# Two-layer attention and feed-forward kernel: in the first layer and in the memory heads, each head transposes its own 64 columns instead of two heads sharing one transpose of 128

## The chip, the cores and the metric

The kernel runs on one core of a Trainium2 chip. The metric is the device time of one execution in microseconds (us); less is better. The profile comes from one execution, and its rows name the engines: PE is TensorE (matmuls and transposes), PEld its weight load, DVE is VectorE, ACT is ScalarE, POOL is GpSimd, SP is the engine that issues most DMAs.

## What is computed

Two transformer layers over 1024 positions of width 1024, all in float32. The first layer ("fox") has 12 causal heads of 64 columns with a decay term, the second ("mla") 12 causal heads of 96 columns; each layer has 4 more heads that attend to a memory of 256 rows. Cut to what the change touches:

```python
def fox_mixer(p, b_f, q_gain, k_gain):
    q, k, v, f = jnp.split(p, [MIX_WIDTH, 2 * MIX_WIDTH, 3 * MIX_WIDTH], axis=-1)
    q = rmsnorm(to_heads(q, N_MIX_HEADS), q_gain) * HEAD_DIM ** -0.5
    k = rmsnorm(to_heads(k, N_MIX_HEADS), k_gain)
    log_f = jax.nn.log_sigmoid(f.astype(jnp.float32) + b_f.astype(jnp.float32))
    cum = lax.cumsum(log_f, axis=1).transpose(0, 2, 1)
    return from_heads(causal_block_attention(q, k, to_heads(v, N_MIX_HEADS), cum))

def memory_cross(qm, k_mem, v_mem, q_gain, k_gain):
    q = rmsnorm(qm.reshape(b, s, N_MEM_HEADS, HEAD_DIM), q_gain) * HEAD_DIM ** -0.5
    k = rmsnorm(k_mem, k_gain)
    ...
# per layer: x = x + concat([o_mix, o_mem]) @ w_out; x = x + conv_ffn(rmsnorm(x), ...)
```

## The kernel before

A float32 product is made of float32r pieces: an operand is split into a high part (a cast) and a low part (operand minus high part), and a product takes two or three matmuls. In a layer the order is: projections, attention, output projection, feed-forward part.

After the projections the queries and keys of two neighbouring heads lie side by side in one tile: `q` and `k` are 128 positions by (8 blocks x 128 columns), columns 0 to 63 of a block belonging to the even head and 64 to 127 to the odd one; `mq` is the same for a pair of memory heads. The scores need them transposed, as QA and KA (high part) and QB and KB (low part), 64 rows by 1024 positions. Each head's `prep` does it in two halves of 512 positions:

- An even head (`load_pair`, `odd` = 0) transposes 4 blocks of 128 x 128 into one PSUM tile `psX`; rows 0 to 63 of it are its own, rows 64 to 127 are the next head's. L519 copies rows 64 to 127 to SBUF, back into the tile that was just read (ScalarE in the first layer, VectorE in the second).
- An odd head reads that copy and transposes nothing.
- `split_T` then scales by the gain: L524 (ScalarE) writes the high part, L525 (VectorE, scalar_tensor_tensor) the low part. For an even head both read `psX`, for an odd head the SBUF copy. The copies are recorded at L83 (ScalarE) and L85 (VectorE), the lines of the helper `copy`.

`psX` is a pool of three PSUM banks. The pass that finds each query's largest score (`maxpass`) uses the same three: PE writes a chunk of scores to `psX`, VectorE reduces it (L299, or L304 with the causal mask) into `mA`, PE transposes `mA`, VectorE negates it into `mrow` (L312) and a DMA puts it into QA. A bank is free again only when VectorE has read it. The score and value matmuls use other banks (`psS`, `psO`); GpSimd subtracts `plo` = `pf` - `ph` (L90) for the low part of the probabilities.

`attention` runs head after head; the preparation and max pass of the next heads are woven between the matmuls of the present one, a pair at a time (`TIMES`). At the end of a pair VectorE takes the reciprocal of the row sums (L394, `rec`), DMAs write it to DRAM and read it back on all partitions (`rrow`), and VectorE multiplies the pair's output by it (L93, `oh`). Each engine works its own queue in order. A scheduler places the instructions of the first layer's attention on each queue; in the second layer's attention PE's order is pinned to the program's.

Of the kernel before, what the change touches and what calls it, by code (L numbers as in the profile page):

```python
# [17 lines left out]
P = 128  # L18
# [7 lines left out]
HD = 64  # L26
# [48 lines left out]
def hybrid_kernel(ctx: ExitStack, tc: tile.TileContext, A, out):  # L75
# [5 lines left out]
    def copy(eng, o, i):  # L81
        if eng == "a":
            nc.scalar.copy(o, i)  # L83
        elif eng == "v":
            nc.vector.tensor_copy(o, i)  # L85
        else:
            nc.gpsimd.tensor_copy(o, i)

    def sub(eng, o, a, b):
        (nc.vector if eng == "v" else nc.gpsimd).tensor_tensor(o, a, b, op=OP.subtract)  # L90
# [14 lines left out]
    def transpose(*a, **k):  # L105
        r = nc.tensor.transpose(*a, **k)  # L106
        return late(r) if pin[0] else r
# [17 lines left out]
    def psX():  # L125
        return psum.tile([P, 512], F32, name="psX", tag="X", bufs=3)
# [19 lines left out]
    def late(ins):  # L146
        return tc.keep_in_program_order(ins)
# [5 lines left out]
    ident = const.tile([P, P], F32, name="ident")  # L153
# [52 lines left out]
    def gc(key, n):  # L206
        i = GC[key]
        return g_cols[0:n, i:i + 1]
# [60 lines left out]
    pl = Pools()  # L269
# [215 lines left out]
    class Head:  # L485
        rows_eng = "vv"
        o = {}
# [13 lines left out]
    def load_T(src, Th, Tl, tl0, tl1, gcol, n, half):  # L501

        px = psX()
        for i in range(4):
            transpose(px[:n, i * P:(i + 1) * P], src(half * 4 + i), ident)
        split_T(px[:n, :], Th, Tl, tl0, tl1, gcol, n, half)

    def load_pair(T, odd, Th, Tl, tl0, tl1, gcol, half):

        hs = slice(half * 512, half * 512 + 512)  # L510
        if odd:
            px = T[0:HD, hs]
        else:
            px = psX()
            for i in range(4):
                t = half * 4 + i
                transpose(px[:, i * P:(i + 1) * P], T[:, t * P:(t + 1) * P], ident)
            copy("v" if pl.layer else "a", T[0:HD, hs], px[HD:P, :])
            px = px[0:HD, :]  # L519
        split_T(px, Th, Tl, tl0, tl1, gcol, HD, half)  # L520

    def split_T(px, Th, Tl, tl0, tl1, gcol, n, half):
        hs = slice(half * 512, half * 512 + 512)
        nc.scalar.activation(Th[0:n, hs], px, AF.Identity, scale=gcol)  # L524
        nc.vector.scalar_tensor_tensor(Tl[tl0:tl1, hs], px, gcol, Th[0:n, hs].bitcast(F32),  # L525
                                       op0=OP.mult, op1=OP.subtract)

    def dup(dst, src):
        nc.sync.dma_start(dst.bitcast(F32), src.bitcast(F32))

    class FoxHead(Head):
# [7 lines left out]
        def prep(self):  # L539
            self.qk_tiles()  # L540
            o = (self.row % 2) * HD
            q, k = self.p
            QA, KA, QB, KB = self.QA, self.KA, self.QB, self.KB

            def qt(half):
                load_pair(q, self.row % 2, QA, QB, 0, 64, gc("fox_q", HD), half)
                if half:
                    dup(QB[64:128, :], QA[0:64, :])

            def kt(half):  # L550
                if not half:
                    dup(KA[64:66, :], self.cum[self.row:self.row + 1])
                load_pair(k, self.row % 2, KA, KB, 64, 128, gc("fox_k", HD), half)
                if half:
                    dup(KB[0:64, :], KA[0:64, :])

            def vs():
                self.vh, self.vl = pl.vtile()
                v = self.pv.rearrange("p (t j) -> p t j", t=NT)[:, :, o:o + HD]
                copy("a", self.vh[:, :, 0:64], v)  # L560
                sub("p" if self.row < 2 else "v", self.vl, v, self.vh[:, :, 0:64].bitcast(F32))

            return [lambda: kt(0), lambda: qt(0), lambda: kt(1), lambda: qt(1), vs]
# [14 lines left out]
    class MemHead(Head):  # L578
# [8 lines left out]
        def prep(self):  # L587
            h = self.h
            q = self.mq[h // 2]
            if self.L:  # L590
                T = pl.qk[h // 2]
                self.QA, self.KA, self.QB, self.KB = T[h % 2], mk[0][:, h], T[2 + h % 2], mk[1][:, h]
                if h not in pl.mem_rows:
                    pl.mem_rows.add(h)
                    copy("p", self.QA[64:66, :], ones1[64:66, 0:1].to_broadcast([2, S]))
            else:
                self.qk_tiles()
            QA, KA, QB, KB = self.QA, self.KA, self.QB, self.KB

            def qt(half):  # L600
                load_pair(q.rearrange("p t d -> p (t d)"), h % 2, QA, QB, 0, 64, gc(f"mem_q{self.L}", HD), half)
                if half:
                    dup(QB[64:128, :], QA[0:64, :])

            def kt():
                g = gc(f"mem_k{self.L}", HD)
                px = psX()
                for t in range(2):
                    transpose(px[:64, t * P:(t + 1) * P], kmem[:, t, h * HD:(h + 1) * HD], ident)
                nc.scalar.activation(KA[0:64, :MEM], px[:64, :256], AF.Identity, scale=g)  # L610
                nc.vector.scalar_tensor_tensor(KB[64:128, :MEM], px[:64, :256], g, KA[0:64, :MEM].bitcast(F32),
                                               op0=OP.mult, op1=OP.subtract)
                if self.L:
                    copy("p", KA[64:67, :MEM], ones1[64:67, 0:1].to_broadcast([3, MEM]))
                copy("p", KA[64:66, :MEM], zero1[64:66, 0:1].to_broadcast([2, MEM]))
                dup(KB[0:64, :MEM], KA[0:64, :MEM])

            return [lambda: qt(0), kt, lambda: qt(1)]

        def v(self, kt):  # L620
# [110 lines left out]
    class FFN:  # L731
# [388 lines left out]
        def down(self, s, k, i, finish):  # L1120
# [13 lines left out]
            for u in range(4):  # L1134
# [5 lines left out]
                if i == N - 1 and u % 2:  # L1140
# [13 lines left out]
    Th, Tl = zip(*((hp.tile([P, ND, P], F32R, name=f"hTh{t}"), hp.tile([P, ND, P], F32R, name=f"hTl{t}"))  # L1154
                   for t in range(NT)))
# [264 lines left out]
    Th, Tl, lat, xt = {}, {}, {}, {}  # L1420
# [258 lines left out]
    for g in range(1, 6):  # L1679
        p = groups[g].pieces()  # L1680
# [37 lines left out]
    for j in range(6):  # L1718
        i, x = divmod(t0 + 0.1 + 0.28 * j, 1.0)
# [48 lines left out]
```

## Time and profile before

| | |
|---|---|
| time, median of 3 runs | 2527.79 us (2522.3 to 2529.79) |
| the profiled execution's own time | 2524.59 us |
| its span, first to last instruction | 2522.8 us |
| mean granted TensorE clock, share of full speed | 0.970 |
| attention of the first layer | about 268 to 512 us |
| attention of the second layer | about 1367 to 1765 us |

The profiled execution's time is its span and 1.8 us around it. A change is to be read against the stage where it happens: the two attention stages are about a quarter of the span, and the rest is projections and feed-forward work that the change does not touch.

### The profile page before, as it was taken

The numbers are of one execution on the slowest core, as the hardware profiler recorded it, in microseconds if no ns is written. First come the engines' busy times: TensorE is split into PE (matmuls) and PEld (weight loads), VectorE is DVE, ScalarE is ACT, GpSimd is POOL, SyncE is SP. The second block draws the span as 40 slices with busy tenths as digits, with TensorE's granted clock in tenths as the row PEclk, the third lists the DMA queues.
The fourth block names the chain that finished last, engine by engine and source line by source line (L and its number), as shares of the span: only waits on it lengthen the run. The fifth ranks groups of instructions, "written<-read, shape, count | busy, mean of one in ns | idle before, by whom it ended". The sixth has DMA issues, their size and how long they took to land.

```text
span 2522.8 us, 32481 instructions
## 1 busy us (share of the span) xinstructions
PE 2369.9 (94%) x11609; PEld 1954.7 (77%) x11609; DVE 1892.6 (75%) x3183; ACT 1209.5 (48%) x2341; POOL 985.3 (39%) x640
## 2 busy tenths in 40 slices
PE   7999899998999999989998798889979999998999
PEld 7999666677788888868888576767868888886887
DVE  7432677757778878789997868774488788778997
ACT  5544678723444444434454555555244444443443
POOL 1221467743233233234332566666132333233342
PEclk9999899999999999999999899989989999999999
DMA  4221121253132232451230101010512222226221
GB/s 143 84 51 27 35 61 47 52 177 109 51 92 76 84 92 76 161 190 52 99 134 11 34 23 27 19 38 22 192 56 84 87 81 84 83 85 242 84 101 67
DMA packets 163651, 208.89 MB, mean 83 GB/s; under 512 B 11175, under 2 KB 124682, under 8 KB 163490
## 3 DMA queue, kind: packets, MB, share of 16 engines
q1 hardware_dynamic: 162054, 206.63, 25.9%
q8 instruction: 92, 1.51, 0.2%
q14 instruction: 69, 0.57, 0.1%
q10 hardware_dynamic: 1436, 0.18, 0.0%
HBM read 153.34 MB, written 39.98 MB: 77 GB/s over the span
## 4 chain that ended last, share of the span: by engine, by line
PE 73%; DVE 17%; issue 3%; DMA 3%; POOL 2%; ACT 2%; SPq 0%; DVEq 0%; ACTq 0%; POOLq 0%
PE psX L102 32%; PE psS L102 25%; PE psO L102 14%; DVE f_op L90 2%; PE psX L106 2%; POOL f_op L90 1%; DVE mA L299 1%; DVE psX L304 1%; DVE f_x L1143 1%; DVE KB L525 1%; DVE f_T L90 1%; DMA rrow<-rec 1%; DVE f_d L90 1%; DVE QB L525 1%; DVE f_S L90 1%
## 5 line engine op out<-in xcount | busy, mean ns | idle before, releaser
L90 POOL TENSOR_TENSOR f_op<-f_S,f_op 128x512 fp32r<-128x512 f32 x184 | 272.0, 1479 | 671.0 <-ACT f_op L83 613.7
L102 PE MATMUL psS<-f_T,f_op 128*128 128x512 f32 x1584 | 382.4, 393 | 7.8 <-DVE f_T L90 5.9
L90 POOL TENSOR_TENSOR plo<-pf,ph 128x1024 fp32r<-128x1024 f32 (+2 forms) x160 | 315.1, 1980 | 158.0 <-ACT pf L343 95.7
L102 PEld LDWEIGHTS psS<-f_T,f_op 128*128 128x128 f32 x1584 | 297.0, 189 | 68.9 <-DVE f_T L90 6.5
L102 PE MATMUL psX<-f_B,f_op 128*128 128x512 f32 x1260 | 296.3, 389 | 0.1
L83 ACT CAST f_op<-f_S 128x512 fp32r<-128x512 f32 x248 | 153.6, 621 | 279.0 <-PE psS L102 109.2
L102 PEld LDWEIGHTS psX<-f_B,f_op 128*128 128x128 f32 x1260 | 236.4, 188 | 49.6 <-issue 0.5
L102 PE MATMUL psS<-f_op 128*128 128x512 f32 x960 | 222.4, 390 | 0.4 <-DVE f_op L90 0.4
L102 PEld LDWEIGHTS psS<-f_op 128*128 128x128 f32 x960 | 180.7, 188 | 39.0 <-DVE f_op L90 1.2
L102 PE MATMUL psX<-f_op 128*128 128x512 f32 x666 | 175.3, 403 | 20.8 <-DVE f_op L90 18.1
L102 PE MATMUL psX<-w_w,hTh 128*128 128x384 f32 (+2 forms) x672 | 167.8, 333 | 2.2 <-ACT hTh L83 2.2
L102 PEld LDWEIGHTS psX<-f_op 128*128 128x128 f32 x666 | 127.9, 194 | 54.0 <-DVE f_op L90 24.2
L898 DVE SCALAR_TENSOR_TENSOR f_v<-f_cv,cw,f_v 128x1023 f32<-128x1023 f32 x88 | 150.9, 1715 | 7.6 <-ACT f_v L896 6.2
L342 ACT ACTIVATE ph<-psS 128x1024 fp32r<-128x1024 f32 (+2 forms) x131 | 112.4, 858 | 90.4 <-PE psS L102 83.4
L83 ACT CAST f_op<-f_raw 128x512 fp32r<-128x512 f32 x148 | 91.4, 621 | 132.3 <-PE psS L102 67.1
L102 PE MATMUL psX<-KA,QA 66*128 66x128 f32 (+4 forms) x320 | 111.0, 395 | 24.5 <-DVE mA L299 10.5
L83 ACT CAST f_op<-f_d 128x512 fp32r<-128x512 f32 x144 | 84.3, 619 | 102.0 <-PE psS L102 35.6
L858 DVE TENSOR_TENSOR f_u<-psS,f_p 128x512 f32<-128x512 f32 x44 | 30.4, 691 | 126.7 <-PE psS L102 126.7
L102 PEld LDWEIGHTS psX<-w_w,hTh 128*128 128x128 f32 x672 | 120.8, 190 | 3.2 <-ACT hTh L83 2.8
L898 DVE SCALAR_TENSOR_TENSOR f_v<-f_cg,cw,f_v 128x1023 f32<-128x1023 f32 x88 | 112.6, 1279 | 11.2 <-ACT f_v L896 11.2
L90 POOL TENSOR_TENSOR f_op<-f_d,f_op 128x512 fp32r<-128x512 f32 x52 | 75.3, 1448 | 115.9 <-ACT f_op L83 115.9
L102 PE MATMUL psS<-QA,KA 67*128 67x512 f32 (+7 forms) x304 | 110.9, 366 | 7.8 <-DMA QA<-mrow 7.8
(379 smaller groups left out, 5698.8 us busy)
## 6 DMA issues: line engine op xcount, KB each, us to landing
f_raw<-in_ffn_w_up_dram SPq DMA_DIRECT2D x88, 512.0 KB
g<-f_v SPq DMA_DIRECT2D x44, 512.0 KB
f_d<-g SPq DMA_DIRECT2D x36, 512.0 KB
f_d<-in_ffn_w_down_dram SPq DMA_DIRECT2D x36, 512.0 KB
w_raw<-in_fox_w_in_dram SPq DMA_DIRECT2D x48, 192.0 KB
rrow<-rec SPq DMA_DIRECT2D x32, 256.0 KB
wo_raw<-in_w_out_dram SPq DMA_DIRECT2D x32, 256.0 KB
xr<-x SPq DMA_DIRECT2D x16, 512.0 KB
```

The source lines that it names most:

```text
L83: nc.scalar.copy(o, i)
L90: (nc.vector if eng == "v" else nc.gpsimd).tensor_tensor(o, a, b, op=OP.subtract)
L102: r = nc.tensor.matmul(*a, **k)
L106: r = nc.tensor.transpose(*a, **k)
L299: nc.vector.tensor_reduce(mA[:, q0:q0 + n], px[:, :n * width].rearrange("p (a b) -> p a b", a=n), axis=AX, op=OP.max)
L304: nc.vector.tensor_tensor_reduce(px[:, off:off + nk], px[:, off:off + nk], mQ[:, 512 - nk:], scale=1.0, scalar=m if on else NEG, op0=OP.ad ...
L342: nc.scalar.activation(ph, ps[:, :w], AF.Exp)
L525: nc.vector.scalar_tensor_tensor(Tl[tl0:tl1, hs], px, gcol, Th[0:n, hs].bitcast(F32), op0=OP.mult, op1=OP.subtract)
L858: nc.vector.tensor_tensor(o, x, y, op=OP.add)
L898: nc.vector.scalar_tensor_tensor(v[:, k:], src[:, :S - k], cw[:, 2 - k, ch:ch + 1], v[:, k:], op0=OP.mult, op1=OP.add)
L1143: nc.vector.tensor_tensor(X[t][:, hs], X[t][:, hs], self.sets[st][v], op=OP.add)
```

## The change

`load_pair` is gone. Every head calls `load_T` (which the second layer's heads of 96 columns already used) with its own 64 columns.

```diff
-    def load_pair(T, odd, Th, Tl, tl0, tl1, gcol, half):
-
-        hs = slice(half * 512, half * 512 + 512)
-        if odd:
-            px = T[0:HD, hs]
-        else:
-            px = psX()
-            for i in range(4):
-                t = half * 4 + i
-                transpose(px[:, i * P:(i + 1) * P], T[:, t * P:(t + 1) * P], ident)
-            copy("v" if pl.layer else "a", T[0:HD, hs], px[HD:P, :])
-            px = px[0:HD, :]
-        split_T(px, Th, Tl, tl0, tl1, gcol, HD, half)
...
 class FoxHead, prep:
-                load_pair(q, self.row % 2, QA, QB, 0, 64, gc("fox_q", HD), half)
+                load_T(lambda t: q[:, t * P + o:t * P + o + HD], QA, QB, 0, 64, gc("fox_q", HD), HD, half)
...
-                load_pair(k, self.row % 2, KA, KB, 64, 128, gc("fox_k", HD), half)
+                load_T(lambda t: k[:, t * P + o:t * P + o + HD], KA, KB, 64, 128, gc("fox_k", HD), HD, half)
...
 class MemHead, prep:
-                load_pair(q.rearrange("p t d -> p (t d)"), h % 2, QA, QB, 0, 64, gc(f"mem_q{self.L}", HD), half)
+                o = h % 2 * HD
+                load_T(lambda t: q[:, t, o:o + HD], QA, QB, 0, 64, gc(f"mem_q{self.L}", HD), HD, half)
```

`load_T`, which is not changed:

```python
    def load_T(src, Th, Tl, tl0, tl1, gcol, n, half):
        px = psX()
        for i in range(4):
            transpose(px[:n, i * P:(i + 1) * P], src(half * 4 + i), ident)
        split_T(px[:n, :], Th, Tl, tl0, tl1, gcol, n, half)
```

Counted over the program: groups of four transposes that feed a head's queries or keys go from 32 (of 128 columns) to 64 (of 64 columns), which is 128 more instructions on PE; 28 copies on ScalarE (24 of the fox heads, 4 of the first layer's memory heads) and 4 on VectorE (second layer) are gone; the 32 pairs of L524 and L525 of odd heads read PSUM where they read SBUF. GpSimd and the DMA queues have as many instructions as before. Lines below the removed function move up by 13 or 14 (L524 becomes L510, L525 becomes L511).

The scheduler also places the first layer's attention anew. Three places show how.

ScalarE at the start of the first layer's attention, before the change (KA_3084 and QA_3083 are the first head's high parts, KA_3076 and QA_3075 the second head's; `junk` are sums of squares of the memory queries, `vh` casts of the values):

```order
L83 COPY k<-psX 64x512
L238 ACTIVATE junk,ssm<-psX 128x64 x3
L83 COPY q<-psX 64x512
L238 ACTIVATE junk,ssm<-psX 128x64
L524 ACTIVATE KA_3084<-psX,g_cols 64x512
L524 ACTIVATE QA_3083<-psX,g_cols 64x512
L83 CAST vh<-v 128x8x64
L524 ACTIVATE KA_3076<-k,g_cols 64x512
L524 ACTIVATE QA_3075<-q,g_cols 64x512
L83 CAST vh<-v 128x8x64 x2
L83 COPY k<-psX 64x512
L524 ACTIVATE KA_3084<-psX,g_cols 64x512
```

The same place with the change:

```order
L510 ACTIVATE KA_3084<-psX,g_cols 64x512
L510 ACTIVATE QA_3083<-psX,g_cols 64x512
L83 CAST vh<-v 128x8x64 x3
L510 ACTIVATE KA_3084<-psX,g_cols 64x512
L238 ACTIVATE junk,ssm<-psO 128x64 x2
L510 ACTIVATE QA_3083<-psX,g_cols 64x512
L238 ACTIVATE junk,ssm<-psO 128x64 x2
L510 ACTIVATE KA_3076<-psX,g_cols 64x512
```

The second head's work has moved behind the first head's; on VectorE its four L525 move in the same way, from between the first head's L525 to behind the first head's `mrow`.

VectorE where the first pair of heads ends, before (KB_3078 and QB_3077 belong to the even head that is being prepared, KB_3082 and QB_3081 to the odd one):

```order
L525 SCALAR_TENSOR_TENSOR QB_3081<-q,g_cols,QA_3079 64x512
L394 RECIPROCAL rec<-sums 16x128
L85 CAST ph<-pf 128x1024
L304 ISA psX,mA<-psX,mQ,mA 128x256
L304 ISA mA 128x1
L525 SCALAR_TENSOR_TENSOR KB_3082<-k,g_cols,KA_3080 64x512
L304 ISA psX,mA<-psX,mQ,mA 128x384
L304 ISA mA 128x1
L525 SCALAR_TENSOR_TENSOR KB_3078<-psX,g_cols,KA_3076 64x512
L304 ISA psX,mA<-psX,mQ,mA 128x512
L304 ISA mA 128x1
L525 SCALAR_TENSOR_TENSOR KB_3082<-k,g_cols,KA_3080 64x512
```

The next row before the change is L93 (`oh`, twice). With the change:

```order
L394 RECIPROCAL rec<-sums 16x128
L85 CAST ph<-pf 128x1024
L511 SCALAR_TENSOR_TENSOR QB_3077<-psX,g_cols,QA_3075 64x512
L299 TENSOR_REDUCE mA<-psX 128x1
L304 ISA psX,mA<-psX,mQ,mA 128x128
L304 ISA mA 128x1
L304 ISA psX,mA<-psX,mQ,mA 128x256
L304 ISA mA 128x1
L511 SCALAR_TENSOR_TENSOR KB_3078<-psX,g_cols,KA_3076 64x512
```

Here four rows of L304 follow, then L93 twice and `mrow`. The odd head's L525 no longer stand at the end of the pair; they come in the next head's stretch, and two L525 stand between `rec` and L93 where three did. At the ends of the second, third and fourth pair the number falls from 2, 3 and 2 to 1, 2 and 1.

PE at the start of the second layer's attention (`mA` is the first memory head's row of maxima, `kmem` the second head's keys, `LTh` the input of the projection of that layer's heads 0 and 1), before:

```order
L106 MATMUL psX<-ident,mA 8x128
L106 MATMUL psX<-ident,kmem 64x128 x2
L102 MATMUL psX<-g_w,LTh 128x192 x2
```

and with the change:

```order
L106 MATMUL psX<-ident,mA 8x128
L106 MATMUL psX<-ident,mq_11813 64x128 x4
L106 MATMUL psX<-ident,kmem 64x128 x2
L106 MATMUL psX<-ident,mq_11813 64x128 x4
L102 MATMUL psX<-g_w,LTh 128x192 x2
```

Two more groups, each with a `psX` bank of its own, stand ahead of the projection.

## Rows read from the trace of the kernel before

**Rows 1.** The page's first part: busy us, share of the span, instructions.

```profile
PE 2369.9 (94%) x11609; PEld 1954.7 (77%) x11609; DVE 1892.6 (75%) x3183; ACT 1209.5 (48%) x2341; POOL 985.3 (39%) x640
```

**Rows 2.** Windows by stage: length, busy us (instructions) by engine, granted clock, DMA.

```profile
core 0: us, PE busy (x) PEld busy (x) DVE busy (x) ACT busy (x) POOL busy (x), PEclk, DMA share, GB/s
268.00:296.00 28.00, 21.27 (x70) 14.46 (x71) 22.69 (x61) 17.16 (x33) 10.09 (x7) 0.63 0.18 38
296.00:500.00 204.00, 189.63 (x1056) 138.22 (x1055) 162.19 (x326) 158.61 (x237) 145.90 (x79) 0.95 0.23 52
1366.00:1412.00 46.00, 33.04 (x167) 26.75 (x165) 37.37 (x85) 23.35 (x48) 20.15 (x19) 0.81 0.16 35
```

**Rows 3.** Windows, PE alone: five ends of pairs, and one stretch between.

```profile
296.00:304.00 8.00, 6.23 (x31) 0.79 0.34 75
332.00:340.00 8.00, 5.84 (x23) 0.79 0.85 191
364.00:376.00 12.00, 9.44 (x40) 0.72 0.58 134
400.00:412.00 12.00, 9.73 (x44) 0.86 0.58 135
436.00:444.00 8.00, 6.44 (x28) 0.79 0.60 143
...
304.00:332.00 28.00, 27.88 (x166) 1.00 0.13 28
```

**Rows 4.** Timeline of PE: groups of transposes, each with the next row.

```profile
288.39 1.05 PE L106 MATMUL psX<-ident,q 128*128 128x128 f32 x4
289.09 0.78 PE L102 MATMUL psX<-KA,QA 66*128 66x512 f32 x1
...
459.11 0.60 PE L106 MATMUL psX<-ident,mq 128*128 128x128 f32 x4
459.47 0.48 PE L102 MATMUL psX<-KA,QA 66*128 66x512 f32 x1
...
464.89 0.38 PE L106 MATMUL psX<-ident,kmem 128*64 128x128 f32 x2
465.03 0.64 PE L102 MATMUL psO<-plo,vh 128*65 128x512 f32 x2
```

**Rows 5.** Groups by line and shape: the copies that go (busy us, mean ns).

```profile
L83 ACT COPY k<-psX 64x512 f32<-64x512 f32 x12 | 7.0, 582 | 12.6 <-PE psX L106 12.4
L83 ACT COPY mq<-psX 64x512 f32<-64x512 f32 x4 | 2.3, 584 | 1.6 <-PE psX L106 1.5
L85 DVE COPY mq<-psX 64x512 f32<-64x512 f32 x4 | 2.8, 694 | 0.1
```

**Rows 6.** Line L525: ns min/median/max by source; then groups by shape.

```profile
L525 DVE SCALAR_TENSOR_TENSOR KB<-psX,g_cols,KA x36: 729/744/748, 268.1 to 1720.2; 96x512 fp32r<-96x512 f32 x24, 64x512 fp32r<-64x512 f32 x12
L525 DVE SCALAR_TENSOR_TENSOR KB<-k,g_cols,KA x12: 745/808/2499, 269.6 to 446.0; 64x512 fp32r<-64x512 f32 x12
...
L525 DVE SCALAR_TENSOR_TENSOR KB<-k,g_cols,KA 64x512 fp32r<-64x512 f32 x12 | 14.4, 1201 | 0.4
L525 DVE SCALAR_TENSOR_TENSOR QB<-q,g_cols,QA 64x512 fp32r<-64x512 f32 x12 | 9.8, 819 | 0.1
L525 DVE SCALAR_TENSOR_TENSOR QB<-mq,g_cols,QA 64x512 fp32r<-64x512 f32 x4 | 7.4, 1860 | 0.3 <-ACT QA L524 0.3
```

**Rows 7.** Timeline of VectorE and PE at the end of the first pair.

```profile
330.96 2.50 DVE L525 SCALAR_TENSOR_TENSOR KB<-k,g_cols,KA 64x512 fp32r<-64x512 f32 x1
333.39 0.61 DVE L304 CUSTOM_DVE_ANT_0 psX<-psX,mQ,mA 128x384 f32<-128x384 f32 x1
...
334.16 0.66 PE L106 MATMUL psX<-ident,q 128*128 128x128 f32 x4 [2.17 <-DVE mA L304]
```

**Rows 8.** Waits of PE from 268 to 296 us: total, times, longest.

```profile
PE psX L102 <- DVE KB L525: 3.5, 1, 3.5
```

**Rows 9.** Chain of waits at the end of the fourth pair: start, us.

```profile
435.01 0.81 DVE rec L394
...
437.74 4.41 DMA rrow<-rec
...
443.13 1.36 DVE oh L93
```

## The prediction

> **What bounds the kernel now.** The page's first part comes first: PE is busy for 94% of the span and VectorE for 75% [rows 1]. That is an average, so the second view is the windows by stage, and there only the stages that the change touches. At the start of the first layer's attention PE is busy for 21.27 of 28 us at a granted clock of 0.63; in the body of that attention for 189.63 of 204 us at 0.95; at the start of the second layer's for 33.04 of 46 us at 0.81 [rows 2]. The third view cuts the body finer. The reader is to see two regimes. Between the ends of pairs PE is full: 27.88 of 28 us at a clock of 1.00 from 304 to 332 us [rows 3], and four more such stretches up to 500 us read the same way, all at 1.00. [...] So work added to PE is paid in full between the ends, and only what shortens the ends, about 20.4 us together, can pay it back. The fourth view, the timeline at one end, says what they wait for: VectorE's L525 for the odd head, which reads the SBUF copy, takes 2.50 us, the masked maximum queued behind it starts only at 333.39, and PE has waited 2.17 us when it goes on at 334.16 [rows 7].
>
> **The change part by part.**
>
> Transposes. 32 groups of four are added. A group holds PE for 459.47 - 459.11 = 0.36 us at full clock, and for 289.09 - 288.39 = 0.70 us at half [rows 4]. Now a transpose has 64 columns, not 128; the two `kmem` transposes, which have 64, hold PE for 0.14 us [rows 4], and since a group of four shows three intervals of 0.11 and a last one of 0.03 (its busy 0.60 less the 0.27 of one, by three), two would take 0.14 with 128 columns as well: narrower ones are not cheaper. So 32 x 0.36 = **+11.5 us**. Bounds: less by what falls into idle PE, 22.4 if all ran at half clock. I take 11.5, since between the ends PE is full at clock 1.00.
>
> Copies. 28 on ScalarE go, 0.58 us each [rows 5], 16.3 us. ScalarE is busy for 158.61 of 204 us [rows 2], and while PE is full its earlier results only wait: **0**. PE's own queue is that cover; at the ends, where it is gone, the gain is in the term for the ends. The four on VectorE in the second layer (0.694 us [rows 5]) are below.
>
> L524 and L525 of odd heads now read PSUM. L525 takes 729 to 748 ns from `psX`, but 745 to 2499 ns from the copy `k` [rows 6]. Summed: `k` 14.4 us where 12 x 0.744 = 8.9 would do, `q` 9.8 for 8.9, the first layer's `mq` 7.4 for 3.0 [rows 6], so 10.8 us of VectorE's time go, nearly all from stretched instructions. [...]
>
> Banks. Each added group takes a `psX` bank until its L525 (0.74 us) has read it, while each even head's bank comes free 0.58 us earlier, as the copy is gone: 32 x 0.16 = 5 us of some 700 us of bank time (three banks, 232 us). I cost it at 0; the two other banks cover it, and without that cover it is 5 us.
>
> The ends of pairs. The odd head's L525 are shorter and stand elsewhere. At the end shown, 2.50 - 0.74 = 1.76 of PE's 2.17 us of waiting is the stretch [rows 6, 7]; over the twelve `k` it is 5.5 us, and I let 4 us of that fall on the five ends. An end that idles less may also not lose the clock: I take two of five, 2/5 of 10.1 = 4 us. So **-8 us**, between 0 (something else keeps VectorE back) and -20.4 (the ends vanish).
>
> The start of the first layer. PE waits 3.5 us for L525 [rows 8] with the second head's L525 standing among the first head's; two of them, at least 0.745 + 0.74 us, leave that place, and a copy with them. Their work comes back in the first head's stretch, so the bounds are 0 and the 6.7 us of idle [rows 2]. I take **-2 us**, nearer to the two instructions.
>
> The last memory heads of the first layer. Four L525 lose 4.4 us in all [rows 6], with the row of maxima and the end of attention behind them; between 0 and -4.4, I take **-1.5 us**, since score and value matmuls of other heads run meanwhile.
>
> The start of the second layer. Four copies of 0.694 us [rows 5] leave VectorE, while PE idles 13 us of 46 [rows 2]; but two groups move ahead of the projection, and each may hold it for a bank, 0.74 us. Between -4.2 (the copies, and the four groups hidden) and +1.5, I take **-1.5 us**.
>
> The DMAs are as many as before, and none moves past another queue.
>
> Sum: 11.5 - 8 - 2 - 1.5 - 1.5 = -1.5 us, against the profiled execution 2524.6 - 1.5 = 2523.1. The median of the three runs shown is 3.2 us above that execution, so for a median I say **2526 us**. A measurement of this kernel can tell about 0.3%, 7.6 us.
>
> **The rivals.**
>
> A, the ends dissolve. For it: at the end shown the stretched instruction is most of the wait, and the clock loss is as large as the idle time, so it goes together with it. Against: at the end from 400 to 412 us PE idles 2.27 us [rows 3] though the timeline has no stretched L525 there. With -20.4 for -8 the sum is -13.9: 2514 us.
>
> B, slower: VectorE comes to L93 too early. From the end of `rec` (435.01 + 0.81 = 435.82) to the landing of `rrow` (437.74 + 4.41 = 442.15) 6.3 us pass, and L93 runs for 1.36 us [rows 9]. With one L525 less in between at each of four ends, VectorE stands waiting at L93, and behind it stand a maximum or `mrow`, for which PE's `mA` transpose waits. It decides when PE runs out of score and value matmuls ahead of `mA` before L93 is done; then the ends give nothing back and each of five gets longer by L93's 1.36 us: 11.5 - 5 + 6.8 = +13.3, so 2541 us. Against: PE has some ten matmuls ahead of `mA` there.
>
> [...]
>
> That the change does not do what it says is excluded by the order: the copies are gone and 128 instructions are added.
>
> **How the numbers follow.** My forecast has 0.45, A 0.28, B 0.22, C 0.05. The forecast's own range, with its terms for the start, the memory heads and the second layer between their bounds, is 2519 to 2534. The range of all reaches to A and to B: 2511 to 2542. Faster by over 0.3% (below 2520) takes nearly all of A and a little of the forecast, 0.31; slower (above 2535) nearly all of B and C and a little of the forecast, 0.26; within 0.3%, 0.43.
>
> **What would show it right or wrong.** PE's busy time in the first layer's attention grows by about 10 us. No L525 with 64 rows takes over 0.75 us. At the ends of pairs the idle time falls from 10.3 to about 6 us and the dips of the clock from five to about three; all gone is A; as before, with VectorE waiting for `rrow` ahead of L93 and PE for `mA`, is B; a clock below 1.00 between the ends is C. A later end of the first layer's output projection for another cause, such as weights loaded later, would make the prediction wrong in a way that no term holds.

## The result, and the profile after

The changed kernel takes 2544.7 us (median of 4 runs, 2540.68 to 2551.9) against 2526.15 us before (median of 4 runs, 2522.3 to 2529.79): a ratio of 1.0081, 95% interval 1.006 to 1.0102, so about 20 us slower. The forecast was 2526 with a range up to 2542. The profiled execution takes 2542.94 us against 2524.59, its span is 18.4 us longer.

The first part of the page of after, against [rows 1]:

```profile
PE 2388.2 (94%) x11737; PEld 1970.6 (78%) x11737; DVE 1888.4 (74%) x3179; ACT 1192.7 (47%) x2313; POOL 979.5 (39%) x640
```

PE has its 128 instructions more and is 18.3 us longer busy; ScalarE is 16.8 us less busy. Where the time went is read from four windows that are cut at the same places of the program: from the first score matmul of the first layer (on KA, QA) to the first feed-forward matmul, that feed-forward part, the second layer up to its feed-forward part, and that part. Columns as in [rows 2]. Before:

```profile
269.70:618.90 349.20, 319.36 (x1588) 236.73 (x1589) 255.11 (x518) 207.32 (x315) 195.01 (x107) 0.94 0.30 84
618.90:1291.30 672.40, 654.13 (x2880) 535.76 (x2879) 564.04 (x698) 301.23 (x458) 236.34 (x153) 0.99 0.30 97
1291.30:1844.70 553.40, 488.00 (x2749) 396.98 (x2747) 391.90 (x916) 275.06 (x518) 271.68 (x184) 0.94 0.17 54
1844.70:2517.40 672.70, 654.09 (x2878) 536.26 (x2876) 556.47 (x670) 291.16 (x440) 226.97 (x149) 0.98 0.29 95
```

After:

```profile
269.70:632.40 362.70, 335.33 (x1700) 250.44 (x1701) 245.05 (x516) 190.75 (x285) 190.29 (x106) 0.93 0.29 81
632.40:1303.80 671.40, 653.76 (x2880) 535.26 (x2879) 564.87 (x700) 301.98 (x458) 234.34 (x153) 0.99 0.30 97
1303.80:1865.10 561.30, 491.25 (x2765) 400.01 (x2763) 394.51 (x913) 274.39 (x518) 270.96 (x184) 0.93 0.17 54
1865.10:2535.80 670.70, 652.67 (x2878) 535.11 (x2876) 557.56 (x669) 291.16 (x440) 227.79 (x149) 0.99 0.29 95
```

The first layer's stage is 13.5 us longer, the second's 7.9, the two feed-forward parts together 3.0 us shorter. In the first layer PE is 16.0 us longer busy; idle time goes only from 29.8 to 27.4 us, and (1 - clock) x length rises from 21.0 to 25.4. So the transposes are paid and the stage as a whole got nothing back for them, though the start did get better. The window that answers to the first of [rows 2]:

```profile
268.00:296.00 28.00, 22.27 (x107) 15.35 (x108) 22.85 (x65) 16.32 (x31) 14.08 (x8) 0.82 0.18 39
```

PE executes 107 instructions there where it had 70, at a clock of 0.82 for 0.63. It is lost again at the ends of pairs. PE at the five ends (the second in two stretches), and between the first and the second, against [rows 3]; columns are length, PE busy (instructions), clock, DMA share, GB/s:

```profile
328.00:336.00 8.00, 5.56 (x34) 1.00 0.42 100
360.00:368.00 8.00, 6.34 (x28) 0.79 0.40 100
372.00:388.00 16.00, 14.26 (x50) 0.57 0.08 18
412.00:428.00 16.00, 14.26 (x60) 0.68 0.08 17
452.00:464.00 12.00, 9.94 (x39) 0.72 0.10 23
488.00:496.00 8.00, 5.91 (x39) 1.00 0.16 34
336.00:360.00 24.00, 23.41 (x141) 1.00 0.16 35
```

The dip at 296 to 304 us is gone. It was not the end of a pair, though [rows 3] counts it as one: the first `rec` comes only at 329.00 us. The fifth end before is this window:

```profile
468.00:480.00 12.00, 10.51 (x63) 1.00 0.49 115
```

The second, third and fourth end now hold PE at a lower clock for longer (0.57 over 16 us at the second, where [rows 3] has 0.72 over 12). Over the five true ends, idle time goes from 10.0 to 11.7 us and (1 - clock) x length from 8.4 to 17.0: by these windows, an estimate, the ends cost PE some 10 us more than before. Where the lead of the start is lost is told by a row of maxima that comes once in each stretch between two ends. Before, behind the first, second and fourth end:

```profile
350.95 0.28 DVE L312 TENSOR_SCALAR mrow<-psX 8x128 fp32r<-8x128 f32 x1 [0.71 <-PE psX L106]
386.55 0.28 DVE L312 TENSOR_SCALAR mrow<-psX 8x128 fp32r<-8x128 f32 x1 [0.55 <-PE psX L106]
456.91 0.28 DVE L312 TENSOR_SCALAR mrow<-psX 8x128 fp32r<-8x128 f32 x1 [0.37 <-PE psX L106]
```

After:

```profile
347.29 0.28 DVE L312 TENSOR_SCALAR mrow<-psX 8x128 fp32r<-8x128 f32 x1
390.57 0.28 DVE L312 TENSOR_SCALAR mrow<-psX 8x128 fp32r<-8x128 f32 x1
468.65 0.28 DVE L312 TENSOR_SCALAR mrow<-psX 8x128 fp32r<-8x128 f32 x1 [0.67 <-PE psX L106]
```

The changed kernel is 3.7 us ahead behind the first end, and 4.0, 9.5 and 11.7 us late behind the second, third and fourth: the loss is made at those three. What VectorE does at the first end is seen in its timeline with PE's (start, us, engine, line):

```profile
329.71 0.27 PE L106 MATMUL psX<-ident,mA 128*8 128x128 f32 x1
330.62 3.19 DVE L93 TENSOR_TENSOR oh<-oh,rrow 128x512 f32<-128x512 f32 x2 [1.28 <-DMA rrow<-rec]
333.72 0.27 DVE L312 TENSOR_SCALAR mrow<-psX 8x128 fp32r<-8x128 f32 x1
334.05 0.44 PE L102 MATMUL psX<-KA,QA 66*128 66x384 f32 x1 [2.44 <-DVE mrow L312]
```

The next head's maxima have been transposed by 329.98, so `mrow` could start. But L93 is ahead of it on VectorE's queue and its `rrow` has not landed: VectorE stands idle for 1.28 us, multiplies for 3.19, and only then writes `mrow`, 3.74 us late. PE's next matmul into `psX` waits 2.44 us for it. The waits of VectorE from 300 to 530 us say that it stands before L93 at every end (total, times, longest):

```profile
DVE oh L93 <- DMA rrow<-rec: 8.3, 5, 2.5
DVE oh L93 <- issue: 1.6, 1, 1.6
```

Six waits: at the five ends above (the one put down to "issue" stands at 409 us) and at the next, near 520 us. What is new is the order on VectorE's queue: in the kernel before, `mrow` stood between `rec` and L93 at four of the five ends, behind L93 only at the first; in the changed kernel it stands behind L93 at all five, and at the second, third and fourth the last masked maximum (L304, 128x512) does too. The third end with the change:

```profile
409.29 2.79 DVE L93 TENSOR_TENSOR oh<-oh,rrow 128x512 f32<-128x512 f32 x2 [1.56 <-issue]
412.00 0.75 DVE L304 CUSTOM_DVE_ANT_0 psX<-psX,mQ,mA 128x512 f32<-128x512 f32 x1
412.86 0.27 PE L106 MATMUL psX<-ident,mA 128*8 128x128 f32 x1 [2.19 <-DVE mA L304]
```

Before, VectorE stood idle ahead of L93 there as well, 1.10 us, but `mrow` was out:

```profile
405.31 0.28 DVE L312 TENSOR_SCALAR mrow<-psX 8x128 fp32r<-8x128 f32 x1
408.82 1.76 DVE L93 TENSOR_TENSOR oh<-oh,rrow 128x512 f32<-128x512 f32 x2 [1.10 <-issue]
```

So PE waits for whatever stands behind L93: for `mrow` at the first and fifth end (2.44 and 1.65 us), for the last maximum at the third and fourth (2.19 and 0.90), and for an L511 behind it at the second and fourth (1.35 and 1.11).

### The profile page after: what moved, and what is told of

Same layout as the page of the kernel before. It is cut to its first block, busy times and chain, and to the rows that moved or that the text cites. A ratio compares the mean times of both kernels' runs of the same rounds, so it can differ in the third digit from the quotient of the medians.

```text
span 2541.2 us, 32695 instructions
## 1 busy us (share of the span) xinstructions
PE 2388.2 (94%) x11737; PEld 1970.6 (78%) x11737; DVE 1888.4 (74%) x3179; ACT 1192.7 (47%) x2313; POOL 979.5 (39%) x640
## 4 chain that ended last, share of the span: by engine, by line
PE 72%; DVE 16%; DMA 4%; issue 3%; ACT 2%; POOL 1%; SPq 1%; DVEq 0%; ACTq 0%; POOLq 0%
PE psX L102 32%; PE psS L102 25%; PE psO L102 14%; PE psX L106 2%; DVE f_op L90 2%; DVE mA L299 1%; DVE f_x L1130 1%; DMA rrow<-rec 1%; POOL f_op L90 1%; DVE oh L93 1%; DMA wo_raw<-in_w_out_dram 1%; DVE f_d L90 1%; DVE psX L304 1%; DVE f_T L90 1%; DVE f_S L90 1%
## 5 line engine op out<-in xcount | busy, mean ns | idle before, releaser
L102 PE MATMUL psX<-f_op 128*128 128x512 f32 x666 | 174.6, 402 | 20.4 <-DVE f_op L90 17.7
L102 PE MATMUL psX<-KA,QA 66*128 66x128 f32 (+4 forms) x320 | 111.4, 398 | 27.7 <-DVE mA L299 10.1
```

What stands on the lines that cost most here:

```text
L102: r = nc.tensor.matmul(*a, **k)
```

## The experiments

Two theories. **The order**: the change loses because VectorE takes L93 ahead of `mrow` and the last maximum, waits there for `rrow`, and PE waits for them. Its rival, **the price**: the added transposes on a full PE are the loss, and the order at the ends is not the matter. Ratios are to runs of the kernel before on the same chip. "First stage" is the window from the first score matmul to the first feed-forward matmul, 349.2 us before and 362.7 after.

An edit in the first layer also lets the scheduler place other instructions of that stage anew, on PE too, so no such run changes one thing alone. Where two kernels got the same order on PE, VectorE, ScalarE and GpSimd in this stage, its length came out alike: 362.7 us in after and 364.5 in e2, 341.6 in e4 and 341.0 in e9.

### e1_twice: added transposes without the change

```diff
-            for i in range(4):
+            for i in (0, 1, 2, 3, 0, 1, 2, 3):     # load_pair, kernel before
```

> The kernel before, in which each of the 32 pair groups of four transposes is done twice into the same bank: 128 more instructions on PE, as in the change, but the copies and everything that the odd heads read stay, and the row of maxima (`mrow`) stays ahead of L93 on VectorE's queue. Theory of the price (the added transposes alone are the loss, since PE is full): +12 to +16 us, most of what the change lost. Theory of the order (the change loses because VectorE takes L93 ahead of `mrow`, and waits there for `rrow`): the transposes partly fall into PE's idle time at the ends, +5 to +10 us.

Measured: 2537.15 us, ratio 1.0052 (1.0034 to 1.0071), 13 us more. Its first stage:

```profile
270.80:629.00 358.20, 329.09 (x1688) 247.86 (x1686) 256.67 (x514) 205.03 (x312) 195.50 (x104) 0.94 0.29 81
```

9.0 us longer, for 28 of the 32 groups: near 28 x 0.36 = 10.1. The time is in the price theory's range, the stage in the other's; the run shows that PE is full enough to pay for the transposes, and doesn't tell the theories apart.

### e2_layer0 and e3_layer1: one layer at a time

The calls of `load_T` as in the change, but in `MemHead` only `if not self.L` (e2), or only `if self.L` with the fox heads as before (e3).

> The change in the first layer alone; the second layer's memory heads keep the pair transposes and VectorE's copies. If the two layers' losses are separate, as the trace of after suggests (the first layer's feed-forward part starts 13.5 us later, the second layer's first `rec` comes another 6.5 us later): +12 to +14 us against before. If the second layer's loss is only a shift that the first one set off: +18 us.

> The change in the second layer's four memory heads alone. Separate losses: +4 to +7 us against before, for only 16 added transposes. By the price of the transposes alone: +1.5 to +3 us. If the second layer's loss was set off by the first: 0 to +1.

Measured: e2 2536.57 us, ratio 1.005 (1.0036 to 1.0065), 13 us more, its first stage 364.5 us; e3 2515.96 us, ratio 0.9971 (0.9957 to 0.9984), 7 us **less**. So the first layer's loss is its own, as expected. The second layer's is not: alone, the same edit gained, which neither theory had. The profile of e3 does not say where. Its second layer's stage and the two feed-forward parts:

```profile
619.20:1287.70 668.50, 650.83 (x2880) 533.65 (x2879) 563.86 (x697) 301.03 (x457) 235.19 (x153) 0.99 0.30 98
1287.70:1843.30 555.60, 494.14 (x2766) 399.76 (x2763) 389.54 (x912) 274.67 (x518) 273.45 (x184) 0.93 0.18 54
1843.30:2512.80 669.50, 651.38 (x2878) 533.55 (x2876) 556.85 (x670) 291.10 (x440) 226.85 (x149) 0.99 0.29 96
```

The stage with the edit is 2.2 us longer than before; the feed-forward parts, which it does not touch, are 3.9 and 3.2 us shorter. What this profile gained is thus not in the stage of the edit.

### e4_mrow_first: the row of maxima first

```diff
-                nc.vector.tensor_scalar(row, px[:8, :P], -1.0, None, op0=OP.mult)
+                pl.mrow = nc.vector.tensor_scalar(row, px[:8, :P], -1.0, None, op0=OP.mult)
...
-            mul("v", raw[:, hs], raw[:, hs], pl.rows[r][:, hs])
+            if L:
+                mul("v", raw[:, hs], raw[:, hs], pl.rows[r][:, hs])
+            else:
+                with tc.issue_after(pl.mrow.ins):
+                    mul("v", raw[:, hs], raw[:, hs], pl.rows[r][:, hs])
```

This is the changed kernel's `final` in the max pass and `norm2`; `issue_after` sets the order on VectorE's queue; what the scheduler then places elsewhere follows from it.

> The changed kernel, with one constraint more in the first layer: L93 is put behind the latest row of maxima (`mrow`) on VectorE's queue. No instruction is added or removed. Theory of the order: PE's waits for `mrow` at the five ends go, and with them the falls of the clock: 6 to 14 us faster than the change, +5 to +12 against before. Theory of the price: what stands at the ends is not the matter, 0 to 2 us faster than the change, +16 to +18 against before.

Measured: 2521.12 us, ratio 0.9988 (0.9975 to 1.0002): the whole loss is gone, some 23 us against the change, more than either theory had. VectorE's and PE's timelines at the first end (line numbers of this kernel), and the first stage:

```profile
332.14 0.28 DVE L312 TENSOR_SCALAR mrow<-psX 8x128 fp32r<-8x128 f32 x1 [0.69 <-PE psX L106]
332.79 3.17 DVE L93 TENSOR_TENSOR oh<-oh,rrow 128x512 f32<-128x512 f32 x2 [0.37 <-DMA rrow<-rec]
...
336.98 0.47 PE L102 MATMUL psX<-KA,QA 66*128 66x512 f32 x1 [0.57 <-DVE QB L515]
```

```profile
271.40:613.00 341.60, 323.36 (x1700) 242.21 (x1700) 242.22 (x513) 188.41 (x285) 188.88 (x104) 0.97 0.31 86
```

L93 still waits and still runs for 3.17 us, but `mrow` is out before it, and PE misses 0.57 us where it missed 2.44. The stage is 21.1 us shorter than in the changed kernel and 7.6 us shorter than before, with the same transposes: idle time 18.2 us for 27.4, (1 - clock) x length 10.2 for 25.4. PE has no wait for VectorE's `mrow` left from 268 to 530 us, where the changed kernel had 4.1 us in two. This is what the order theory said, by more than its size; what the scheduler moved on PE along with it is in the 21.1 us too and was not separated.

### e5_before_mrow_last and e6_before_mrow_first: the order on the kernel before

e5 puts `mrow` behind the latest L93 in the same way (the constraint is on the other instruction), and gives the normalisation earlier places in the program (`"norm": (2, 8, 9)` for `(7, 24, 27)`), without which L93 is not yet traced when `mrow` is. e6 has e4's constraint.

> The kernel before, with the order of the change forced on it at the ends of the first layer's pairs: the row of maxima (`mrow`) stands behind L93 at all five ends, where it stood ahead of it at four; pair transposes and copies are as before. Theory of the order: PE waits for `mrow` at every end as in the changed kernel, +8 to +20 us against before. Theory of the price (the order is not the matter): within 2 us of before.

> The kernel before with the constraint of the run that put the row of maxima first: here it can change the first end alone, since at the other four `mrow` stands ahead of L93 anyway. Theory of the order: 0 to -3 us; so the 20 us that the constraint gave the changed kernel are what the change's own order cost. If the constraint were good for something else, before would gain as much: -10 us or more.

Measured: e5 2552.99 us, ratio 1.0119 (1.0099 to 1.014), 30 us more, beyond the expected 20; e6 2524.3 us, ratio 1.0006 (0.9995 to 1.0016), no change. PE's waits in e5's attention and its first stage:

```profile
PE psX L102 <- DVE mrow L313: 13.8, 5, 3.8
```

```profile
271.40:649.00 377.60, 328.90 (x1589) 242.26 (x1589) 248.91 (x522) 208.81 (x318) 194.06 (x108) 0.89 0.28 77
```

13.8 us of waiting for `mrow` in five waits, 28.4 us more for the stage, and a clock of 0.89: without one added transpose, e5 loses more than the change did. Not all of it is VectorE's order. At the first end, where L93 was ahead of `mrow` before as well, the scheduler also put PE's transpose of `mA` ahead of the ten value matmuls that stood before it, and PE waits there for `mrow`, 2.15 us; the earlier places of the normalisation were not tried alone. Where `mrow` is ahead already at four ends, as in e6, the constraint is worth nothing.

### e10_norm_on_gpsimd: the wait on another queue

```diff
-            mul("v", raw[:, hs], raw[:, hs], pl.rows[r][:, hs])
+            mul("v" if L else "p", raw[:, hs], raw[:, hs], pl.rows[r][:, hs])     # changed kernel
```

> The changed kernel with L93 in the first layer (the multiplication by `rrow`) on GpSimd, not on VectorE; no order is forced. Theory of the order (what stands behind a waiting L93 on VectorE is what PE lacks): nothing waits for `rrow` on VectorE any more, the ends shrink as in the run with the row of maxima first: 8 to 18 us faster than the change; less if `plo`, which now waits behind L93 on GpSimd, is missed by PE. Theory of the price: within 3 us of the change.

Measured: 2535.11 us, ratio 1.0046 (1.0029 to 1.0062), about 9 us less than the change. First stage, and what PE waited for most from 270 to 530 us:

```profile
269.80:624.10 354.30, 328.39 (x1700) 245.92 (x1700) 233.82 (x498) 190.39 (x284) 210.76 (x121) 0.95 0.30 83
```

```profile
PE psO L102 <- POOL plo L90: 4.2, 4, 2.5
```

8.4 us shorter than in the changed kernel, at the lower edge of what was expected: the wait for `rrow` now stands ahead of `plo`, and PE waits for that.

### e11_first_and_twice: the price where the ends are short

e4, with each head's own group done twice (`for i in (0, 1, 2, 3) * (1 if n > HD else 2)` in `load_T`).

> The changed kernel with the row of maxima first, and each head's own group of four transposes done twice into the same bank: 64 groups more, 256 instructions. It prices a group where the ends are short. At the full clock a group holds PE for 0.36 us: 64 x 0.36 = 23 us slower than with single groups (+18 to +24). If the groups fall into idle time of PE: under +12.

Measured: 2556.75 us, ratio 1.0129 (1.0111 to 1.0146), 36 us more than e4 by the ratios, beyond both readings; its first stage is 375.3 us, 33.7 more. The added groups are not hidden in this stage. The run does not price one, though: 56 x 0.36 is 20.2 us, and the stage's idle time also rose, from 18.2 to 25.9 us, and its clock fell from 0.97 to 0.95.

### e7_rope_gpsimd, e8_best_pair, e9_layer0_mrow_first, e12_projection_first: the second layer

In the trace of after PE's longest wait in the second layer's stage, 5.6 us, is at the start of its attention. VectorE, GpSimd and PE there:

```profile
1407.58 4.69 POOL L90 TENSOR_TENSOR plo<-pf,ph 128x1024 fp32r<-128x1024 f32 x2
1407.63 2.44 DVE L93 TENSOR_TENSOR rope<-gq,cos 128x128 f32<-128x128 f32 x1
1409.99 2.42 DVE L93 TENSOR_TENSOR rope<-gq,sin 128x128 f32<-128x128 f32 x1
...
1413.29 0.27 DVE L312 TENSOR_SCALAR mrow<-psX 8x128 fp32r<-8x128 f32 x1
...
1413.62 1.06 PE L106 MATMUL psX<-ident,mq 128*64 128x128 f32 x4 [5.57 <-DVE mrow L312]
```

The same place before, where these products ran ahead of GpSimd's `plo`:

```profile
1391.98 0.28 DVE L93 TENSOR_TENSOR rope<-gq,cos 128x128 f32<-128x128 f32 x1
1392.17 0.55 DVE L93 TENSOR_TENSOR rope<-gq,sin 128x128 f32<-128x128 f32 x1
...
1399.79 1.11 PE L106 MATMUL psX<-ident,mq 128*128 128x128 f32 x4 [4.33 <-DVE mrow L312]
```

PE waited for this `mrow` before, too, 4.33 us: the wait grew by 1.24 us, and the stage by 7.9.

e7 is e4 with these two products on GpSimd:

> The changed kernel with the row of maxima first in the first layer, and in the second layer the two products of `rope` for the second half of heads 0 and 1 on GpSimd, not on VectorE, where they took 2.43 and 2.42 us beside GpSimd's two `plo` (0.28 and 0.55 us alone, in the trace of before) ahead of the second memory head's `mrow`. If those 4 us hold PE up: 3 to 6 us faster than the same kernel without this edit, at the second layer's first `rec` too. If PE waits there for something else anyway: 0 to 1 us.

e8 is e3 with `mrow` first in the first layer:

> Pair transposes in the first layer, the change in the second layer alone (6.8 us faster than before when run by itself), and the row of maxima first in the first layer. Theory of the order: -6 to -10 us against before, the sum of the two. If the second layer's start depends on where VectorE's work happens to fall rather than on the edit: anything from -8 to +4.

e9 is e2 with `mrow` first:

> The change in the first layer alone, with the row of maxima first there; the second layer keeps its pair transposes and copies. The first layer gave -7.5 us in the run with the change in both layers and the row of maxima first. If the second layer's part of the change costs something of its own (its attention took 555 to 561 us with it, 553 to 555 in three runs of four without): -6 to -10 us against before, 3 to 6 us faster than the change in both layers with the row first. If it costs nothing: the same as that run, -1 to -3.

e12 is e4 with the projection, and the steps of heads 0 and 1 that follow it in the list, ahead of the second memory head's groups (index 10 of `fill` becomes 7):

> The changed kernel with the row of maxima first in the first layer, and in the second layer the projection ahead of the second memory head's groups of transposes on PE, as in the kernel before (the change put two of these groups ahead of it). The change in both layers with the row first stood at 0.9988 of before, with the first layer alone changed at 0.9971, so the second layer's edit costs about 4 us there. If the two groups ahead of the projection are the cost: 0.996 to 0.998 of before, level with the first layer alone. If the cost is in what VectorE has to do there in either order: 0.998 to 1.000, as without this edit.

Measured: e7 2521.37 us, ratio 0.9994 (0.9981 to 1.0006), as e4. PE's waits at that place in e7:

```profile
PE psX L102 <- DVE mA L299: 4.1, 1, 4.1
PE psX L106 <- DVE mrow L312: 2.9, 1, 2.9
```

The wait for `mrow`, 5.6 us in e4 as in after, is halved, and a wait for the maxima takes its place. e8: 2525.97 us, 1.0012 (1.0002 to 1.0022), so what e3 gained is not there beside the constraint, which by itself (e6) costs nothing that can be measured. e9: 2516.56 us, 0.9971 (0.9958 to 0.9985), level with e3; it is 4 us below e4, but their intervals overlap.

e12: 2520.0 us, 0.9989 (0.998 to 0.9999), as e4: the two groups ahead of the projection, which the prediction feared, are not shown to be the cost.

The second layer's stage took 553.4 to 560.1 us in five profiles without its edit (before, e2, e5, e6, e9) and 555.6 to 561.3 in seven with it (after, e3, e4, e7, e8, e10, e12): means of 555.7 and 559.0, 3.3 us apart. One profile does not tell that much: in e2 and e6 all four engines have the same instructions in the same order in this stage, and it took 555.3 and 560.1 us. By the times the edit costs 8 us beside the change of the first layer (1.0081 less 1.0050), 4 us in e4 against e9, 1.5 in e8 against e6, and gains 7 in e3; the 4 and the 1.5 are within what the intervals leave open.

## Why the prediction was wrong

**The step that failed** is "The ends of pairs": "The odd head's L525 are shorter and stand elsewhere ... I let 4 us of that fall on the five ends", "So -8 us". The stretched L525 did go, but VectorE met L93 before the last maximum and `mrow`, and the ends took some 10 us more instead of 8 less (the windows above). That was rival B's mechanism, at 0.22, and the prediction's own sign of it, idle time at the ends as before with VectorE waiting for `rrow`, is what the trace has. What was held against it, "PE has some ten matmuls ahead of `mA` there", was too short: at the third end with the change, eight stand between the next head's transposes and `mA`, and PE was through them 2.19 us before the maximum was out. B's size is partly luck. Its +13.3 us is a sum over both layers, and that the first layer alone lost 13.5 does not bear out its parts: L93 was put at 1.36 us and took 3.19, 1.29, 2.79, 2.37 and 2.67 us at the five ends, and the rise of (1 - clock) x length at the ends, 17.0 us for 8.4 by the windows, is in no term of it. The listing of VectorE's queue in the section on the change has L93 ahead of `mrow` at the first end; the prediction did not go on to the other ends, where the order had turned round. That the constraint on this order takes the loss away (e4), that moving L93 to another queue takes part of it away (e10), and that the reverse constraint brings a loss (e5) all fit; how much of each is the order itself and how much the scheduler's other moves is open.

**The clock's part of that -8**, 2/5 of 10.1 = 4 us: the 10.3 us of idle time and the 10.1 us of clock are sums over the five windows of [rows 3], of length less busy time and of (1 - clock) x length, together the 20.4. That an end which idles less keeps its clock, and two of five at that, was the author's guess, and no run shows it. What was measured goes both ways: in the changed kernel 2.44 and 2.09 us of idle time came at a clock of 1.00 (328 to 336 and 488 to 496 us) and 1.74 us at 0.57 (372 to 388 us), while over the stage from the changed kernel to e4 both fell, idle time from 27.4 to 18.2 us and (1 - clock) x length from 25.4 to 10.2.

**Transposes, +11.5**: in line with e1, 9.0 us for 28 groups in the first stage and 13 us (8.6 to 18) over the whole; e11 shows that the same groups can cost more where the order changes with them.

**L525 from PSUM**: right. In after (line L511; the heads in question are among the 64-row forms):

```profile
L511 DVE SCALAR_TENSOR_TENSOR QB<-psX,g_cols,QA x60: 722/738/748, 268.9 to 1740.8; 64x512 fp32r<-64x512 f32 x36, 96x512 fp32r<-96x512 f32 x24
L511 DVE SCALAR_TENSOR_TENSOR KB<-psX,g_cols,KA x52: 729/744/749, 268.1 to 1740.1; 64x512 fp32r<-64x512 f32 x28, 96x512 fp32r<-96x512 f32 x24
```

None is over 749 ns, where the copy's went to 2499 [rows 6]. In the kernel before, all eleven L525 over 0.75 us ran, in whole or in part, beside a `plo`, a `vl` or an `otl` of GpSimd. Two `plo` run from 330.56 to 335.69 us, for one: the L525 from `k` that starts at 330.96 takes 2.50 us, the one from `psX` at 334.13 takes 0.74. The two products of `rope` above took 2.44 and 2.42 us beside `plo`, and 0.28 and 0.55 in the kernel before, where they ran ahead of it. The 745 ns in the prediction is the fastest from the copy `k`; from `q`, in SBUF too, it is 732, and the fastest of after, from PSUM, is 722. So L525 was no faster from SBUF than from PSUM here.

**Rival A, the ends dissolve**: it is what the change can do once `mrow` is ahead. e4's first stage is 7.6 us shorter than before though it pays for 28 groups, 10.1 us: so, as an estimate, some 18 us came back from the start and the ends, near the 20.4 that the prediction had as the bound for the ends and 2 for the start. **Rival C**, a clock below 1.00 between the ends, did not come: from 336 to 360 us the clock is 1.00, and e4, with the same transposes, has 0.97 over the stage.

**The start, -2**: right in sign, and by 296 us PE has executed 37 instructions more. The first `rec` comes at 323.49 us, 5.5 earlier than before; the dip at 296 to 304 us, which the prediction had put among the ends, is part of that.

**The forecast's own range**, 2519 to 2534, does not follow from its bounds: 11.5 - 8 - 6.7 - 4.4 - 4.2 and 11.5 - 8 + 1.5 added to the median of 2527.8 give 2516 to 2533.

**The second layer, -1.5**: wrong for the changed kernel, +7.9 us in its trace and 8 by the times. It is a second step that failed, and the reason is open. The two products of `rope` took 4.0 us longer beside `plo` than before, ahead of it, but PE's wait there was only 1.24 us longer than before, and with the products on GpSimd the wait moved (e7); putting the projection first brought nothing (e12). VectorE's instructions there stand in another order in most kernels tried, and the edit's worth by the times goes from -7 to +8 us; that the one makes the other was not shown, and two kernels with the same order differ by 4.8 us in this stage (e2, e6). The copies (0), the banks (0) and the last memory heads (-1.5) were not tried by themselves. Why the scheduler puts L93 first after the change was not tried either.

## What to carry to other kernels

On VectorE's queue an L93 that waited 1.1 to 2.5 us for a DMA also held back the maximum and the row of maxima behind it, which PE needed. After any change that lets a scheduler place work anew, look at each repeated place for what has come to stand behind such a wait, and who waits for that, before counting what the change saves. Here a constraint on the order of L93 and `mrow`, with what the scheduler moved along with it, was worth some 20 us, twice what the added transposes cost. With it, the change in the first layer alone is 0.3% faster than the kernel before (0.9971, 0.9958 to 0.9985).

## What the hardware showed that was not expected

The feed-forward parts took 672.4 and 672.7 us before, 671.4 and 670.7 after and 668.5 and 669.5 in e3, whose queues hold the same instructions in the same order as before up to the end of the first of them. So two executions of the same work differ by 3.9 us in a stage of 670, as e2 and e6 do by 4.8 us in the second layer's, and a cause must be read from waits and not from a stage's length alone.
